# Key norms as two 288-token halves, later store and reload of the solved blocks, and three longer projection stretches in a Hymba/RWKV-7 layer

## The chip, the cores and the metric

The kernel runs on one core of one Trainium2 chip. The metric is device microseconds of one execution. A core has TensorE (PE, the matmuls, with its weight loads shown apart as PEld), VectorE (DVE), ScalarE (ACT), GpSimd (POOL) and SyncE (SP), which in this kernel issues nearly all DMAs. Each of these works through a queue of its own, and engines wait for one another by semaphores. Matmul results go to PSUM, which here is eight banks of 512 float32 per partition.

## The reference, cut to what matters

One layer on 512 tokens plus 16 meta tokens, width 2048:

```python
hn = rmsnorm(h_res, norm_in_g)
P = hn @ w_in                       # 65 column tiles of 128: r k v g (8 each), lora, B C h gc (8 each)
# group A, 16 heads of 64: token shift, decay by a low-rank path, then
kk = (k * k_k) / max(norm(k * k_k over the head), 1e-12)
S_t = S_{t-1} diag(w_t) - (S_{t-1} kk_t)(kk_t * a_t)^T + v_t k_t^T ;  y_t = S_t r_t
y_a = (groupnorm(y) + bonus) * silu(g_r)
# group B: y_b = Bg * causal_conv3(Cg * hc) * silu(g_c)
out = rmsnorm(h_res + concat(y_a, y_b) @ w_out, norm_f_g)[16:]
```

The recurrence over tokens is computed in nine chunks of 64 positions (the 16 meta tokens are padded to a chunk, so a head pair has 576 columns). Within a chunk it needs the inverse of a unit triangular 64x64 matrix for each head and chunk.

## The kernel before, in words

**Projections as filler.** All matmuls that matter in size are float32 products split into high and low parts: three matmuls (high by high, low by high, high by low) for each 128x128 weight tile. `mains` (from L449) is a generator that yields after each projection matmul of the 65 column tiles, in the order of `plan` (L105): lora k0 r0 v0 k1 r1 v1 g0 g1 C0 h0 B0 gc0, then for each later pair of head pairs k r v k r v g g C h B gc, and at the end C h B gc for i = 4 to 7. A column tile uses four quarters of weights (512 columns each); a `wr` load (L134) brings two quarters, ACT casts the high part `wh` (L126), and DVE (even quarters) or POOL (odd quarters) subtracts to get the low part `wl` (L127). Three raw buffers and six buffers each for high and low parts let this run up to six quarters ahead of PE.

**The host clock.** The order of PE's instructions is written out by hand. `fill(ns)` lets the generator run until so many nanoseconds of projection have been emitted, by a price of 0.43 ns a column; the dictionary `FW` holds these stretches. `until(key)` lets it run until a named tile is complete. `later(ns, fn)` emits a DMA when the same clock has advanced by `ns`; it is put behind the latest weight load on SP. The instructions of DVE, ACT, POOL and SP are put in order by the compiler's scheduler, by priority and by its own idea of when operands are there; `ahead()` and the splitting of weights raise the priority.

**One head pair (`prepare`, from L577).** It runs until k of the pair is complete, makes decays (`low_rank`), the operands `ar` and `bk`, and then products of 64 by 128 per head and chunk (`gram`, L631, the Gram blocks), masked on DVE into `gt`. The squares of k (split in `sqh`, `sql`) are summed over each head by a matmul with a two-column 0/1 matrix (L663, L664): these are the key norms `n2`, first 512 columns into a PSUM tile `zn`, then 64 columns into the free end of the ninth Gram block's tile `ze[0]`. Then follows `zb` (L666, L667), a 128-column product for the bonus term. ACT copies the norms to SBUF (L670). They go to DRAM and come back as 72 rows of 16 (`nd`), and the 16x16 diagonal blocks of the triangular matrices come the same way (`d`). DVE inverts all of them in some 40 small steps that end at L739 (`y`). `y` is stored to DRAM (L754) and read back transposed as `xT` and `xo` (L745, L746, both in `load_inverse`). The Gram blocks, keys and values go to `opd` in DRAM meanwhile (`bt`, `vs`, `gt` stashes, L567).

**Two head pairs together (`invert`, from L781).** After a stretch of `FW["solve"]` (`FW["solve_first"]` for the first two head pairs) the 16x16 inverses are combined to 32x32 and to 64x64: a DVE transpose `xn` for each head pair (L794), 64 small matmuls `t` (L801), an ACT copy `ts`, matmuls `z` (L815, L817), DVE copies into `xT` and transposes `xm`, matmuls `t2` (L841), ACT copies `tm`, matmuls `z2` (L856, L860), DVE copies into `xT` (L866), each step followed by a stretch of projection. Then `put_inverse` stores them. After the last two head pairs the stretch is `FW["begin"]`, and the recurrence follows (`recur`, from L888): per chunk `ct` loads (L883), matmuls `rz`, `zs`, `zy`, three stretches of projection, a norm. What is left of the projections runs after it beside the loads of the mixed rows (`split_mix`), and the output projection `o` (L1087) ends the kernel.

**C, h, B, gc** of group B: `u` (POOL, L401) multiplies C by h, ACT takes the first tap of the convolution (`cv`, L403), DVE the other two (L405), POOL multiplies by B (L413), DVE gates (L362, L419).

Of the kernel before, what the change touches and what calls it, by code (L numbers as in the profile page):

```python
# [9 lines left out]
F32 = mybir.dt.float32  # L10
# [8 lines left out]
P = 128  # L19
DM = 2048  # L20
KT = DM // P
SEQ = 512
META = 16
L = SEQ + META
CH = 64
NCH = SEQ // CH + 1
LP = NCH * CH
# [13 lines left out]


FW = dict(
    evac=34, start=1062, lora=2200, gram=8000, gram_b=13500, gram2=5500, misc=2000, v=2000, vt=1000, solve=22500, solve_first=26000,
    tr=3200, lev=3000, cp=4200, out=1500, begin=17000, p=2900, u=2900, s=5200, last=3700, mix=2600,
)


# [28 lines left out]
def hymba_kernel(ctx: ExitStack, tc: tile.TileContext, xt, xtok, w_in, w_out, pv, lup, cst, msk, gf, out):  # L77
    nc = tc.nc
    ctx.enter_context(tc.manual_schedule(engines={mybir.EngineType.PE}))
    cp = ctx.enter_context(tc.tile_pool(name="cp", bufs=1))  # L80
# [16 lines left out]
    def col(off, i=0):  # L97
        return pvt[:, off + i : off + i + 1]
# [56 lines left out]
    pz = ph1.enter_context(tc.tile_pool(name="pz", bufs=2, space=PSUM))  # L155
    pi = ph1.enter_context(tc.tile_pool(name="pi", bufs=1, space=PSUM))
# [5 lines left out]
    def tr(name, dt=F32):  # L162
        return cq.tile([P, LP], dt, tag="tr", name=name, bufs=5)
# [118 lines left out]
    for b in range(2):  # L282
# [5 lines left out]
        out=omm, in0=pvt[:, V_MU : V_MU + 33], scalar1=-1.0, scalar2=1.0, op0=ALU.mult, op1=ALU.add  # L288
    )
    for d, off in (  # L290
# [4 lines left out]
            out=d, in0=pvt[:, off : off + 8], scalar1=0.5, scalar2=None, op0=ALU.mult  # L295
        )
    nc.vector.tensor_scalar(
        out=hv[:, 4], in0=pvt[:, V_KA : V_KA + 8], scalar1=-0.5, scalar2=1.0, op0=ALU.mult, op1=ALU.add
# [183 lines left out]
    def later(ns, fn):  # L482
        pending.append((clock[0] + ns, fn))
        pending.sort(key=lambda e: e[0])
# [30 lines left out]
    def low_rank(i, j, up, w0, name, pad):  # L515
        t = tr(name)
        nc.gpsimd.memset(t[:, META:CH], pad)
        hi, lo = up
        for a, b in ((0, 272), (272, L)):
            z = pz.tile([P, b - a], F32, tag="tz", name=f"{name}_{a}")  # L520
            nc.tensor.matmul(z, hi[:, j], la[:, j, a:b], start=True, stop=False)
            nc.tensor.matmul(z, lo[:, j], la[:, j, a:b], start=False, stop=True)
            with tc.high_priority(offset=AHEAD):
                if a == 0:
                    nc.scalar.activation(t[:, 0:META], z[:, 0:META], AF.Tanh, bias=w0, scale=0.5)
                    nc.scalar.activation(t[:, CH : 5 * CH], z[:, META:272], AF.Tanh, bias=w0, scale=0.5)
                else:
                    nc.scalar.activation(t[:, 5 * CH : LP], z, AF.Tanh, bias=w0, scale=0.5)
            fill(FW["lora"])
        return t  # L530
# [5 lines left out]
    def c3(t):  # L536
        return t.rearrange("p (c s) -> p c s", s=CH)
# [39 lines left out]
    def prepare(i):  # L577
        p = i % 2
# [8 lines left out]
        tz = low_rank(i, 0, up, hv[:, 0, i : i + 1], f"tz{i}", -1.0)  # L587
# [12 lines left out]
            out=bk[:, :, 0], in0=c3(k), scalar=hv[:, 2, i : i + 1], in1=c3(te), op0=ALU.mult, op1=ALU.mult  # L600
# [3 lines left out]
            out=ta, in0=ta, scalar1=hv[:, 3, i : i + 1], scalar2=hv[:, 4, i : i + 1], op0=ALU.mult, op1=ALU.add  # L604
        )
        nc.vector.scalar_tensor_tensor(
            out=ar[:, :, 0], in0=c3(k), scalar=col(V_KK, i), in1=e1[:, :, 0:CH], op0=ALU.mult, op1=ALU.mult
# [8 lines left out]
            out=ar[:, 1:NCH, 1], in0=c3(r), in1=e1[:, 1:NCH, 1 : CH + 1], op=ALU.mult  # L616
        )
        nc.vector.scalar_tensor_tensor(
            out=r, in0=r, scalar=hv[:, 5, i : i + 1], in1=ta[:, CH:LP], op0=ALU.mult, op1=ALU.mult
# [9 lines left out]
        def gram(z, c, c0):  # L629
            for h, hs, ho in heads:  # L630
                nc.tensor.matmul(  # L631
                    z[h][:, c - c0],
                    bk[hs, c, h : h + 2, :].rearrange("p a s -> p (a s)"),
                    ar[hs, c].rearrange("p a s -> p (a s)"),
                    start=True, stop=True,
                )
# [17 lines left out]
        masked(zc, 4, 8)  # L654
        fill(FW["gram2"])

        ze = [pz.tile([P, P + CH], F32, tag="tz", name=f"g{i}_8_{h}") for h in range(2)]
        gram([z[:, 0:P].unsqueeze(1) for z in ze], 8, 8)
        n2 = tr(f"n2{i}")
        zn = pi.tile([2, SEQ], F32, tag="misc", name=f"n2_{i}")  # L660
        zs = ((zn, 0, SEQ), (ze[0][0:2, P : P + CH], SEQ, LP))
        for z, a, b in zs:
            nc.tensor.matmul(z, ones[:, P : P + 2], sqh[:, a:b], start=True, stop=False)  # L663
            nc.tensor.matmul(z, ones[:, P : P + 2], sql[:, a:b], start=False, stop=True)  # L664
# [17 lines left out]
        sx = scr_x[i % 2]  # L682
# [4 lines left out]
        def blocks(t):  # L687
            return bass.AP(tensor=t.tensor, offset=t.offset, ap=[[BLK, 8 * NCH], [CH, 16], [1, 16]])
# [15 lines left out]
        y = cq.tile([NB, 256], F32, tag="y", name=f"y{i}").rearrange("p (s t) -> p s t", t=16)  # L704
# [14 lines left out]
        for m in (2, 4, 8):  # L719
            for b in range(16 // (2 * m)):  # L720
# [4 lines left out]
                    out=pq,  # L725
# [5 lines left out]
                    out=tq.rearrange("p (i j) -> p i j", i=m), in_=pq, op=ALU.add, axis=AX.X  # L731
                )
                nc.vector.tensor_tensor(
                    out=pq,
# [16 lines left out]
                    ),  # L751
                )

        later(20500 if p else 29000, lambda: nc.sync.dma_start(blocks(sx), y))  # L754
        later(22500 if p else 33000, load_inverse)

        for h, hs, ho in heads:
            for b in range(2):
# [6 lines left out]
        v = got["v", i]  # L765
# [244 lines left out]
    for i in range(0, NPAIR, 2):  # L1010
        invert([prepare(i), prepare(i + 1)])
# [56 lines left out]
    last = [[pw.tile([P, 512], F32R, name=f"wlast{a}{j}") for j in range(NL)] for a in range(2)]  # L1068
# [105 lines left out]
    with tc.manual_schedule(engines={mybir.EngineType.DVE, mybir.EngineType.Activation, mybir.EngineType.Pool}):  # L1174
# [9 lines left out]
        for part in range(2):  # L1184
# [3 lines left out]
            if part == 0:  # L1188
                finish(2)
                nc.vector.tensor_tensor(  # L1190
                    out=fv[:, 3, 0:1], in0=fv[:, 3, 0:1], in1=ssq[:, 3, 3:4], op=ALU.add
# [60 lines left out]
```

## Time and profile before

| | |
|---|---|
| median of 3 runs | 1050.98 us (1050.79 to 1051.12) |
| the profiled execution's own time | 1051.02 us |
| its span, first to last instruction | 1049.2 us |
| mean granted TensorE clock | 0.994 |
| projections of `w_in` end, `o` begins | about 861.8 us from the span's start |
| share of 16 DMA engines' time taken by SP's and ACT's queue | 54.6% |

A row of the page's first part gives busy time, share and number of instructions of each engine. A row of the waits gives engine and line, what it waited for, and the total, the number and the longest in us. A row for one tile gives the number of instructions, the least, median and longest duration in ns, and first and last start. A row of the timeline gives start, duration (both us), engine, line, operation, the tiles written and read, and, in brackets, the idle time before it and what ended that. A row of the chain gives start, duration, engine and line. The starts of matmuls are those at which PE took them up; their ends are modelled, so the pace is read from start to start. The SP rows are the issue of a DMA, not its transfer.

### The profile page before, as it was taken

Reading aid. Unit: us, or ns where it says so; the run is one execution under the profiler, and the core shown is the slowest. Engines: PE = TensorE matmul, PEld = TensorE weight load, DVE = VectorE, ACT = ScalarE, POOL = GpSimd, SP = SyncE. Lnnn points to the kernel's source line nnn. Section 1 sums busy time; section 2 is a strip of 40 time slices with the busy share of each in tenths; the row PEclk is TensorE's granted clock in tenths of the full one; section 3 lists DMA queues with packets and bytes.
Section 4 is the critical chain, followed back from the end, with each engine's and each line's share of the span. In section 5 each row is a group of like instructions: output and inputs, shape, how many; then the busy total and the mean of one; then the engine's idle time right before and its main releaser. Section 6 shows DMA issues by size and latency. Waiting matters only on the chain.

```text
span 1049.2 us, 23744 instructions
## 1 busy us (share of the span) xinstructions
PE 1031.6 (98%) x9845; PEld 940.8 (90%) x9845; DVE 580.1 (55%) x1088; ACT 360.0 (34%) x666; POOL 311.1 (30%) x315
## 2 busy tenths in 40 slices
PE   8999998999999999999999999999999999999996
PEld 6999996999998999989999988889898988888885
DVE  6786855569754669753768752444555761212222
ACT  7554313433322434332443232222233342323232
POOL 0132613323222323222323131223233232424132
PEclk8999999999999999999999999999999999999998
DMA  8436565464763273853374748777654958323314
GB/s 292 141 101 166 128 160 145 114 159 103 193 182 114 82 193 84 202 159 114 104 171 103 196 144 291 241 219 221 211 135 150 286 182 296 101 86 95 101 61 161
DMA packets 183404, 167.48 MB, mean 160 GB/s; under 512 B 121472, under 2 KB 143744, under 8 KB 182912
## 3 DMA queue, kind: packets, MB, share of 16 engines
q1 hardware_dynamic: 182720, 164.90, 54.6%
q8 instruction: 77, 1.26, 0.5%
q10 hardware_dynamic: 576, 1.07, 0.3%
q14 instruction: 31, 0.25, 0.1%
HBM read 129.05 MB, written 36.88 MB: 158 GB/s over the span
## 4 chain that ended last, share of the span: by engine, by line
PE 94%; DMA 2%; issue 1%; DVE 1%; POOL 0%; SPq 0%; ACT 0%; DVEq 0%; ACTq 0%; POOLq 0%
PE o L1087 17%; PE ps_v L315 9%; PE ps_g L315 9%; PE ps_k L315 9%; PE ps_gc L315 9%; PE ps_r L315 8%; PE ps_B L315 8%; PE ps_C L315 8%; PE ps_h L315 8%; PE g L631 2%; DMA wq<-in_w_in_dram 1%; PE zs L954 1%; PE zy L958 1%; PE ps_lora L315 1%; PE rz L902 1%
## 5 line engine op out<-in xcount | busy, mean ns | idle before, releaser
L127 POOL TENSOR_TENSOR wl<-wr,wh 128x512 fp32r<-128x512 f32 x150 | 208.8, 1392 | 460.0 <-ACT wh L126 439.6
L126 ACT CAST wh<-wr 128x512 fp32r<-128x512 f32 x312 | 190.0, 618 | 411.7 <-PE o L1087 93.0
L127 DVE TENSOR_TENSOR wl<-wr,wh 128x512 fp32r<-128x512 f32 x162 | 121.7, 756 | 224.4 <-ACT wh L126 223.2
L1087 PE MATMUL o<-wh,m 128*128 128x512 f32 (+1 forms) x484 | 145.2, 384 | 0.0
L1087 PEld LDWEIGHTS o<-wh,m 128*128 128x128 f32 x484 | 89.6, 188 | 21.3
L1087 PE MATMUL o<-wl,m 128*128 128x512 f32 (+1 forms) x242 | 92.6, 389 | 0.0
L315 PE MATMUL ps_h<-xh,wh 128*128 128x258 f32 (+1 forms) x256 | 72.7, 284 | 0.6 <-issue 0.6
L315 PE MATMUL ps_k<-xh,wh 128*128 128x264 f32 x256 | 73.2, 286 | 0.0
L315 PE MATMUL ps_v<-xh,wh 128*128 128x264 f32 x256 | 73.2, 286 | 0.0
L315 PE MATMUL ps_k<-xl,wh 128*128 128x264 f32 x256 | 73.1, 285 | 0.0
L315 PE MATMUL ps_k<-xh,wl 128*128 128x264 f32 x256 | 72.9, 285 | 0.0
L315 PE MATMUL ps_r<-xh,wh 128*128 128x258 f32 (+1 forms) x256 | 72.2, 282 | 0.7 <-ACT wh L225 0.7
L315 PE MATMUL ps_v<-xh,wl 128*128 128x264 f32 x256 | 72.7, 284 | 0.0
L315 PE MATMUL ps_v<-xl,wh 128*128 128x264 f32 x256 | 72.7, 284 | 0.0
L315 PE MATMUL ps_C<-xh,wh 128*128 128x258 f32 (+1 forms) x256 | 72.5, 283 | 0.0
L315 PE MATMUL ps_g<-xl,wh 128*128 128x258 f32 (+1 forms) x256 | 72.4, 283 | 0.0
L315 PE MATMUL ps_h<-xl,wh 128*128 128x258 f32 (+1 forms) x256 | 72.3, 283 | 0.0
L315 PE MATMUL ps_C<-xl,wh 128*128 128x258 f32 (+1 forms) x256 | 72.3, 282 | 0.0
L315 PE MATMUL ps_r<-xh,wl 128*128 128x258 f32 (+1 forms) x256 | 72.1, 282 | 0.0
L315 PE MATMUL ps_r<-xl,wh 128*128 128x258 f32 (+1 forms) x256 | 72.0, 281 | 0.0
L315 PE MATMUL ps_g<-xh,wh 128*128 128x258 f32 (+1 forms) x256 | 71.9, 281 | 0.0
L315 PE MATMUL ps_C<-xh,wl 128*128 128x258 f32 (+1 forms) x256 | 71.9, 281 | 0.0
(274 smaller groups left out, 2715.9 us busy)
## 6 DMA issues: line engine op xcount, KB each, us to landing
wr<-in_w_in_dram SPq DMA_DIRECT2D x127, 512.0 KB
ct<-opd SPq DMA_DIRECT2D x64, 288.0 KB
wr<-in_w_out_dram SPq DMA_DIRECT2D x32, 512.0 KB
opd<-ar SPq DMA_DIRECT2D x8, 576.0 KB
opd<-gt SPq DMA_DIRECT2D x16, 288.0 KB
opd<-bt SPq DMA_DIRECT2D x64, 64.0 KB
xres<-in_xtok_dram SPq DMA_DIRECT2D x4, 768.0 KB
out_dram<-xres SPq DMA_DIRECT2D x6, 512.0 KB
```

The costliest lines, as they stand in the source:

```text
L126: nc.scalar.copy(hi, rq)
L127: eng.tensor_tensor(out=lo, in0=rq, in1=hi.bitcast(F32), op=ALU.subtract)
L315: nc.tensor.matmul(ps[r], ww[:, w], xx[:, kt, a:b], start=(kt == 0 and n == 0), stop=(kt == KT - 1 and n == 2))
L631: nc.tensor.matmul(z[h][:, c - c0], bk[hs, c, h : h + 2, :].rearrange("p a s -> p (a s)"), ar[hs, c].rearrange("p a s -> p (a s)"), start= ...
L902: nc.tensor.matmul(z[e][ho if e else hs, 0, k], t[hs, o : o + CH], t[hs, O_V : O_V + CH] if part else st[hs, 4 * e + k], start=(part == 0 ...
L954: nc.tensor.matmul(d[hs, j], w, x[hs], start=(a == 0), stop=(a == b - 1))
L958: nc.tensor.matmul(d[ho, j], t[hs, o : o + CH], x[hs], start=(a == 0), stop=(a == b - 1))
L1087: nc.tensor.matmul(ps[t + p], mm[:, tk], ww[:, o], start=(jj == 0 and q == 0), stop=(jj == KT - 1 and q == 2))
```

## The change

Three things. The key norms are made in two halves of 288 columns, and the second half goes into the ninth Gram block's tile, which grows from 128+64 to 128+288 columns. The stretches `solve`, `solve_first` and `begin` grow by 2000, 4000 and 2500 ns of the host clock. The store of `y` and the reload of `xT` and `xo` of the odd head pairs are due 2000 ns later, those of head pair 1 by 5000 ns.

```diff
-    evac=34, start=1062, lora=2200, gram=8000, gram_b=13500, gram2=5500, misc=2000, v=2000, vt=1000, solve=22500, solve_first=26000,
-    tr=3200, lev=3000, cp=4200, out=1500, begin=17000, p=2900, u=2900, s=5200, last=3700, mix=2600,
+    evac=34, start=1062, lora=2200, gram=8000, gram_b=13500, gram2=5500, misc=2000, v=2000, vt=1000, solve=24500, solve_first=30000,
+    tr=3200, lev=3000, cp=4200, out=1500, begin=19500, p=2900, u=2900, s=5200, last=3700, mix=2600,
...
-        ze = [pz.tile([P, P + CH], F32, tag="tz", name=f"g{i}_8_{h}") for h in range(2)]
+        ze = [pz.tile([P, P + 288 * (1 - h)], F32, tag="tz", name=f"g{i}_8_{h}") for h in range(2)]
         gram([z[:, 0:P].unsqueeze(1) for z in ze], 8, 8)
         n2 = tr(f"n2{i}")
-        zn = pi.tile([2, SEQ], F32, tag="misc", name=f"n2_{i}")
-        zs = ((zn, 0, SEQ), (ze[0][0:2, P : P + CH], SEQ, LP))
+        zn = pi.tile([2, 288], F32, tag="misc", name=f"n2_{i}")
+        zs = ((zn, 0, 288), (ze[0][0:2, P : P + 288], 288, LP))
         for z, a, b in zs:
             nc.tensor.matmul(z, ones[:, P : P + 2], sqh[:, a:b], start=True, stop=False)
             nc.tensor.matmul(z, ones[:, P : P + 2], sql[:, a:b], start=False, stop=True)
...
-        later(20500 if p else 29000, lambda: nc.sync.dma_start(blocks(sx), y))
-        later(22500 if p else 33000, load_inverse)
+        later((25500 if i == 1 else 22500) if p else 29000, lambda: nc.sync.dma_start(blocks(sx), y))
+        later((27500 if i == 1 else 24500) if p else 33000, load_inverse)
```

## The prediction

> **What bounds the kernel now.** I read the page's busy shares first, then PE's own waits, longest first, then the timelines around the longest of them.
>
> ```profile
> PE 1031.6 (98%) x9845; PEld 940.8 (90%) x9845; DVE 580.1 (55%) x1088; ACT 360.0 (34%) x666; POOL 311.1 (30%) x315
> ```
>
> PE is occupied nearly throughout, so the time is PE's work plus the places where it stands. The change leaves the number of columns that PE multiplies as it is. It can only win what PE loses in standing or in imperfect overlap, and it can lose by making new waits. PE's waits, of which I leave out those of the first 50 us and one of 0.6 us:
>
> ```profile
> PE ps_B L315 <- DVE wl L127: 1.6, 1, 1.6
> ...
> PE ps_gc L315 <- DVE wl L127: 0.9, 1, 0.9
> ...
> PE t L801 <- DVE xn L794: 0.5, 1, 0.5
> PE rz L902 <- DMA ct<-opd: 0.5, 1, 0.5
> ```
>
> Four waits, each once, 3.5 us together. Three of them lie close together in the first inversion; PE's timeline there:
>
> ```profile
> 157.83 0.39 PE L315 MATMUL ps_B<-xl,wh 128*128 128x512 f32 x1
> 159.81 0.50 PE L315 MATMUL ps_B<-xh,wl 128*128 128x512 f32 x1 [1.59 <-DVE wl L127]
> ...
> 165.25 0.39 PE L315 MATMUL ps_gc<-xl,wh 128*128 128x512 f32 x1
> 166.56 0.50 PE L315 MATMUL ps_gc<-xh,wl 128*128 128x512 f32 x1 [0.92 <-DVE wl L127]
> ...
> 168.88 0.69 PE L801 MATMUL t<-xn,gt 64*64 64x64 f32 x32 [0.50 <-DVE xn L794]
> 169.50 0.50 PE L315 MATMUL ps_gc<-xh,wh 128*128 128x512 f32 x1
> 169.84 0.39 PE L315 MATMUL ps_gc<-xl,wh 128*128 128x512 f32 x1
> ```
>
> The reader is to see the restart too: after a wait the next matmul follows 0.34 us later (169.50 to 169.84), where the usual distance for 512 columns is 0.23 us (zb_l below, 85.36 to 85.59). A wait so costs 0.11 us more than its bracket says. Who made PE wait is in the queues of ACT, POOL, DVE and SP at this place:
>
> ```profile
> 155.78 0.72 ACT L403 ACTIVATE cv<-u,pvt 128x512 f32<-128x512 f32 x1 [11.78 <-POOL u L401]
> 156.41 2.17 ACT L126 CAST wh<-wr 128x512 fp32r<-128x512 f32 x4
> ```
> ```profile
> 153.58 2.17 POOL L401 TENSOR_TENSOR u<-u,hh 128x514 f32<-128x514 f32 x1 [10.80 <-DVE hh L334]
> ```
> ```profile
> 150.82 0.43 DVE L334 TENSOR_TENSOR hh<-ps_h,rs 128x258 f32<-128x258 f32 x1 [3.09 <-PE ps_h L315]
> ...
> 153.09 0.41 DVE L334 TENSOR_TENSOR hh<-ps_h,rs 128x256 f32<-128x256 f32 x1
> ...
> 158.00 1.76 DVE L127 TENSOR_TENSOR wl<-wr,wh 128x512 fp32r<-128x512 f32 x1
> 165.21 0.69 DVE L334 TENSOR_TENSOR b<-ps_B,rs 128x512 f32<-128x512 f32 x1 [5.46 <-PE ps_B L315]
> 165.82 2.38 DVE L127 TENSOR_TENSOR wl<-wr,wh 128x512 fp32r<-128x512 f32 x2
> 168.12 0.70 DVE L794 STREAM_TRANSPOSE xn<-xT 128x512 f32<-128x512 f32 x1
> ```
> ```profile
> 155.32 0.30 SPq L754 DMA_DIRECT2D sx<-y  x1
> 155.72 0.51 SPq L134 DMA_DIRECT2D wr<-in_w_in_dram  x1
> ```
>
> **First wait (1.59).** Four casts stand on ACT behind the convolution's first tap `cv`, which stands 11.78 us for POOL's `u`, which waits for the second half of `hh`; that half came 2.3 us after the first because steps of the `y` chain stood between them on DVE. **Second (0.92).** The next `wl` stands on DVE behind `b`, which cannot start before PE is through with B. **Third (0.50).** The transposition of the second head pair stands behind those two `wl`.
>
> The queue that the change touches is SP's. It stood for `y` before the store:
>
> ```profile
> SPq L754 <- DVE y L739: 14.3, 4, 7.4
> ```
>
> Here the longest case, 7.4 us, ended with the store at 155.32, and the weight load behind it went out at 155.72. But the weights of the first two waits had been loaded before (the casts at 156.41 waited for ACT's own queue, not for a DMA). So the visible block on SP is not what PE waited for in the first two waits. I hold this against the easy reading of the profile.
>
> **The norms.** Columns: 2x512 and 2x64 before, 4x288 after, 1152 both times. PE around the first of eight:
>
> ```profile
> 84.75 0.39 PE L664 MATMUL n<-sq_l,ones 128*2 128x512 f32 x1
> 84.98 0.19 PE L663 MATMUL g<-sq_h,ones 128*2 128x64 f32 x1
> ...
> 85.04 0.48 PE L666 MATMUL zb<-rk_h,ones 128*128 128x512 f32 x1
> 85.36 0.40 PE L667 MATMUL zb<-rk_l,ones 128*128 128x512 f32 x1
> 85.59 0.28 PE L315 MATMUL ps_r<-xl,wh 128*128 128x258 f32 x1
> ```
>
> The two 64-column matmuls take 0.06 us together (84.98 to 85.04), in proportion to the 0.23 us of 512 columns. But `zb` with the high part takes 0.32 us to the next start, 0.09 more than its twin: 0.06 us of matmul is not long enough to hide the load of its 128 weight columns. A 288-column matmul lasts 0.23 x 288/512 = 0.13 us, so after the change the load is hidden as it is behind every 258-column projection. Win: about 0.08 us x 8 = **0.6 us**, bounds 0 and 0.7.
>
> A rule speaks against this term. The Trainium skill, "TensorE: Matmul & The Clock Gate", section "Back-to-back issue gap", gives for a single warm matmul a gap of N/2.4 + 2.5 ns. By it the four cost 2x215.8 + 2x29.2 = 490 ns before and 4x122.5 = 490 ns after: nothing won, and the sum below would come to 1049.8. It does not describe this trace, whose step from zb to zb is 320 and not 216 ns.
>
> ACT copies the norms:
>
> ```profile
> L670 ACT COPY n<-n x8: 575/576/576, 85.2 to 572.1; 2x512 f32<-2x512 f32 x8
> L670 ACT COPY n<-g x8: 197/197/197, 85.7 to 572.5; 2x64 f32<-2x64 f32 x8
> ```
>
> The three figures are the least, the median and the longest in ns. (576-197)/448 is 0.85 ns a column, so 387 ns for 288: 774 against 773 ns. The first can start 0.2 us earlier, the masking of the shared bank ends about where it did. Nothing on PE: 0.
>
> **The longer stretches.** They move projections from behind a point to ahead of it. Until where? The next `prepare` begins with `until` k. Rows of the chain:
>
> ```profile
> 182.40 0.68 PE t L841 x50
> ...
> 194.28 1.31 PE ps_r L315 x11
> ...
> 318.00 0.68 PE t L841 x50
> ...
> 345.38 1.31 PE ps_r L315 x11
> ...
> 791.91 2.55 PE ps_h L315 x20
> ...
> 861.77 177.06 PE o L1087 x798
> ```
>
> After `t2` at 182.40 the first inversion has `lev` 3000 and `out` 1500 of the host clock left; 10.57 us of that clock (48x512x0.43) are about 48 x 0.23 = 11.1 us of PE, a factor of 1.05. That and 1.6 us of small products end near 189. k2 is complete at 194.28, so `until` already supplies some 5 us; the added 4000 (4.2 us) only shorten that. In the next inversion 345.38 - 318.00 leaves some 20 us for an added 2.1; the third is alike. So the first three additions are swallowed and prepare(2), (4) and (6) stay where they are. Only the last, 2000 + 2500, moves the recurrence, by 4.7 us of projection. The tail has room: the recurrence ends near 791.9 (the last two rows) and `o` starts at 861.8, of which `last` and `mix` need 4x3.7+8x2.6 = 35.6, so some 30 us stay. Cost 0.
>
> What comes closer together: `z2` of the first inversion to the first low-rank product, by 4 us to some 5. That product needs a PSUM bank which eight DVE copies must have read:
>
> ```profile
> 322.87 2.40 DVE L866 COPY xT<-z 32x128 f32<-32x128 f32 x8 [0.48 <-PE z L860]
> ```
>
> 2.4 + 1 us of matmuls and waiting fit in; if two `wl` come between (2.38 above), PE stands up to 1 us. I take 0.
>
> **Store and reload.** For head pair 1 the store moves on SP from ahead of the load of the next weights to behind that and the one after; SP no longer stands for `y`, and the weight load of 155.72 can go out near 148. The second load waits for a raw buffer that is split at 159.8, so the store goes at about 160, the reload at 162 to 165, landing near 167. The `t` stage moves by 4.2 us to about 172. So `xn` is no longer last: the third wait, 0.50 + 0.11 = **0.6 us**, goes. In the other pairs store, reload and use move together.
>
> The **first two waits** (1.59 + 0.92 + 2x0.11 = 2.7 us) hang on the order in which the scheduler put `cv`, `b` and the splits; what comes before the store in program order is unchanged by the edit, so I take that they stay: 0, the other bound -2.7.
>
> **The start of the recurrence.**
>
> ```profile
> 644.78 0.33 PE L902 MATMUL rz<-ct 64*64 64x64 f32 x4 [0.48 <-DMA ct<-opd]
> ```
>
> 4.7 us more projection ahead of `rz` cover this wait: 0.48 + 0.11 = **0.6 us**.
>
> **Sum.** -0.6 - 0.6 - 0.6 = -1.8 us on the profiled execution's 1051.0 (span 1049.2 and 1.8 around it), which is within 0.1 of the median of 1050.98: **1049.2 us**. A measurement of this kernel tells about 0.2%, 2.1 us, from no change, so this forecast lies just inside "same".
>
> **Rivals.**
> A: the new order on SP also changes the scheduler's order on ACT and DVE, and the first two waits go as well. For it: `wl` at 165.82 waited for nothing but its place. Against: the queue ahead of the store is the same. 1049.2 - 2.7 = **1046.5**.
> B: the edit doesn't do what it says: the waits around the first inversion only change places, `xn` or a split late by as much, and just the norms and the recurrence's start are won, or the norms alone: 1049.8 to **1050.4**.
> C, slower: in the three later inversions, which have no PE wait now, the `t` stage stands 2 us later beside h and B. If the copies and transposes of the inversion come ahead of `hh` there, the splits fall behind `cv` on ACT as in the first one. Price: the first wait, 1.7 us, in each of three: 1049.2 + 5.1 = **1054.3**. It decides as soon as `cv` stands so long that ACT's six quarters of lead (16.6 us of PE) are used up; all three must do so, or two of them with the second wait as well (5.4), for a slower verdict.
>
> **How the numbers follow.** Forecast 0.42 (own range 1048.3 to 1050.0, of which 0.13 falls below 1048.9), A 0.30, B 0.08, C 0.20. Faster by over 0.2%: 0.13 + 0.30 = 0.43. Within: 0.29 + 0.08 = 0.37. Slower: 0.20. The range takes in A with 0.5 of margin and half of C: 1046.0 to 1053.5.
>
> **What would show it.** `zb` of high parts followed after 0.23 us by its twin, eight times. No bracket at `rz` of chunk 0 and none at `t`. L754 gone from SP's long waits, the weight load behind it near 148. If ps_B and ps_gc still wait for `wl`, the forecast holds; if not, A. New waits of ps_C, ps_h, ps_B or ps_gc after 290 us mean C. Wrong would be the whole if the recurrence moved by some 13 us instead of 4.7, or if PE's steps of the projections changed.

## The result and the profile after

The changed kernel takes 1062.9 us (median of 4 runs, 1062.2 to 1064.44) against 1050.88 us for the one before. The ratio is 1.0117, with a 95% interval of 1.0099 to 1.0134: slower by 1.2%. The profiled execution's span is 1061.5 us, 12.3 more than before.

PE's waits in the changed kernel; the rows left out belong to the first 50 us, the last gives the start of the recurrence:

```profile
PE t L801 <- DVE xn L794: 11.8, 4, 7.7
...
PE ps_gc L315 <- DVE wl L127: 0.9, 1, 0.9
PE ps_B L315 <- DVE wl L127: 0.6, 1, 0.6
PE rz L902 <- DMA ct<-opd: 0.4, 1, 0.4
```

The wait for `xn` was there once with 0.5 us. It is there four times now, once in each inversion, with 11.8 us, and the longest is 7.7. So the place of the loss is the first small matmuls of the inversions. To see how much each costs, the chain of the two kernels is compared at the same instructions. Two rows of the kernel before that the prediction does not show, each the start of a head pair's Gram blocks:

```profile
118.02 1.99 PE g L631 x32
...
260.81 1.20 PE g L631 x17
```

and the rows of the changed kernel:

```profile
118.74 1.99 PE g L631 x32
...
203.00 1.31 PE ps_r L315 x11
...
269.39 1.99 PE g L631 x32
...
355.45 1.31 PE ps_r L315 x11
...
874.06 177.06 PE o L1087 x798
```

From the Gram blocks at 118 to the end of k2 (the start of that `ps_r`) it was 194.28 - 118.02 = 76.3 us and is 84.3: +8.0, in the first inversion. From 260.81 to 345.38 it was 84.6 and is 86.1: +1.5, in the second; the third has the same distance, and the fourth the same wait. The span had lost 0.7 before 118 us, in the loads at the start, which the change does not touch (PE's first projections start at 21.92, 21.09 before). After `o` begins nothing differs.

**The first inversion.** SP's queue in the changed kernel. In the text I count the weight loads from 0, two for each column tile; the load at 159.48 is w26.

```profile
159.48 0.35 SPq L134 DMA_DIRECT2D wr<-in_w_in_dram  x1
159.88 0.40 SPq L754 DMA_DIRECT2D sx<-y  x1
169.03 2.05 SPq L134 DMA_DIRECT2D wr<-in_w_in_dram  x2
171.13 0.60 SPq L745 DMA_DIRECT2D xT<-sx  x1
...
173.12 0.64 SPq L746 DMA_DIRECT2D xo<-sx  x1
173.86 1.73 SPq L134 DMA_DIRECT2D wr<-in_w_in_dram  x2
```

The store goes at 159.88, and the reload could follow some 2.6 us later, as it did in the kernel before, whose store went at 155.32:

```profile
157.90 0.60 SPq L745 DMA_DIRECT2D xT<-sx  x1
```

But in the changed kernel w27 and w28 stand ahead of it, and w27 has to wait for a raw buffer: SP stands from 160.3 to 169.0 with the reload behind it. The reload is issued from 171.13 to 173.76, and then shares the DMA engines with four weight loads. DVE and PE:

```profile
179.24 0.71 DVE L794 STREAM_TRANSPOSE xn<-xT 128x512 f32<-128x512 f32 x1 [5.14 <-DMA xT<-sx]
```
```profile
180.01 1.13 PE L801 MATMUL t<-xn,gt 64*64 64x64 f32 x32 [7.73 <-DVE xn L794]
...
182.09 0.63 PE L315 MATMUL ps_gc<-xh,wl 128*128 128x512 f32 x1
182.51 0.63 PE L315 MATMUL ps_gc<-xh,wh 128*128 128x512 f32 x1
```

After the wait the matmuls are 0.42 us apart (182.09 to 182.51), not 0.23. The windows of the same stretch show why; the columns are us, busy time of PE, PEld, DVE, ACT and POOL, granted clock, DMA share, GB/s:

```profile
171.60:180.00 8.40, 0.68 (x33) 0.54 (x32) 1.40 (x2) 1.14 (x2) 1.84 (x2) 0.84 1.00 243
180.00:184.20 4.20, 4.19 (x40) 3.45 (x41) 0.00 (x0) 1.08 (x2) 0.00 (x0) 0.51 0.14 54
184.20:190.00 5.80, 5.80 (x88) 4.71 (x87) 3.56 (x8) 1.20 (x2) 0.00 (x0) 1.00 0.02 4
```

During the wait the DMA engines are full (1.00), and after it the granted clock is 0.51 for 4.2 us. Seven matmuls then cost 0.2 us more each and the 32 of `t` 0.4 more, some 1.8 us on top of the 7.7. Less the 1.6 us by which the old waits shrank (`ps_B` from 1.59 to 0.60, `t` without its 0.50 and the restart behind it) that is 7.9 of the 8.0.

The Trainium skill, "TensorE: Matmul & The Clock Gate", section "What's actually happening", says that the array falls to half its clock after an idle window of about 3.4 us and returns after a busy one. The trace agrees: 0.51 behind 8.4 us of near idleness, and no such slow rows behind the waits of 0.6 to 1.4 us (the granted clock is 1.00 from 160 to 166 us and from 317 to 320).

**The later inversions.** DVE in the second one before the change and after it:

```profile
302.84 0.70 DVE L794 STREAM_TRANSPOSE xn<-xT 128x512 f32<-128x512 f32 x1
306.62 0.69 DVE L127 TENSOR_TENSOR wl<-wr,wh 128x512 fp32r<-128x512 f32 x1 [3.08 <-ACT wh L126]
307.23 0.42 DVE L334 TENSOR_TENSOR hh<-ps_h,rs 128x258 f32<-128x258 f32 x1
```
```profile
314.21 0.43 DVE L334 TENSOR_TENSOR hh<-ps_h,rs 128x258 f32<-128x258 f32 x1 [7.49 <-PE ps_h L315]
314.55 1.28 DVE L127 TENSOR_TENSOR wl<-wr,wh 128x512 fp32r<-128x512 f32 x2
315.75 0.70 DVE L794 STREAM_TRANSPOSE xn<-xT 128x512 f32<-128x512 f32 x1
```
```profile
316.51 0.69 PE L801 MATMUL t<-xn,gt 64*64 64x64 f32 x32 [1.36 <-DVE xn L794]
```

Before, the transposition stood ahead of `hh`. Now it stands behind the first half of `hh`, for which DVE waits 7.49 us until PE is through with that half of h, and behind two splits. The reload had landed: its last part is issued by 307.9, and from 314 to 316 the DMA engines have nothing to move (share 0.00). PE stands 1.36 us in each of three inversions.

### The profile page after: what moved, and what is told of

The parts are those of the page before. It is cut to its first block, busy times and chain, and to the rows that moved or that the text cites. A ratio compares the mean times of both kernels' runs of the same rounds, so it can differ in the third digit from the quotient of the medians.

```text
span 1061.5 us, 23736 instructions
## 1 busy us (share of the span) xinstructions
PE 1034.3 (97%) x9845; PEld 943.7 (89%) x9845; DVE 575.5 (54%) x1088; ACT 360.2 (34%) x666; POOL 302.3 (28%) x315
## 3 DMA queue, kind: packets, MB, share of 16 engines
q10 hardware_dynamic: 576, 1.07, 0.3%
## 4 chain that ended last, share of the span: by engine, by line
PE 90%; DMA 3%; issue 2%; DVE 1%; SPq 1%; POOL 1%; ACT 0%; DVEq 0%; POOLq 0%; ACTq 0%
PE o L1087 17%; PE ps_v L315 9%; PE ps_k L315 9%; PE ps_g L315 8%; PE ps_r L315 8%; PE ps_gc L315 8%; PE ps_h L315 8%; PE ps_B L315 8%; PE ps_C L315 7%; PE g L631 2%; DMA wq<-in_w_in_dram 1%; PE zs L954 1%; PE zy L958 1%; PE ps_lora L315 1%; PE rz L902 1%
## 5 line engine op out<-in xcount | busy, mean ns | idle before, releaser
L127 POOL TENSOR_TENSOR wl<-wr,wh 128x512 fp32r<-128x512 f32 x150 | 201.0, 1340 | 459.7 <-ACT wh L126 441.4
L315 PE MATMUL ps_h<-xh,wl 128*128 128x258 f32 (+1 forms) x256 | 72.2, 282 | 0.0
```

The lines of the kernel that those rows point to most:

```text
L127: eng.tensor_tensor(out=lo, in0=rq, in1=hi.bitcast(F32), op=ALU.subtract)
L315: nc.tensor.matmul(ps[r], ww[:, w], xx[:, kt, a:b], start=(kt == 0 and n == 0), stop=(kt == KT - 1 and n == 2))
```

## The experiments

My theory after the traces: two places in queues make the loss, the reload's on SP (first inversion) and the transposition's on DVE (the others), and the norms are a small win. Rivals: (1) the norms' longer hold of the Gram block's bank upsets the solve; (2) the longer stretch costs by itself; (3) the cost grows in proportion to the delay. Ratios are to the kernel before on the same chip, where its median was 1051.39 us (e1 to e4), 1051.88 (e5 to e8) or 1052.0 (e9 to e11).

**e1, norms alone.** The three lines of the norms from the diff above, constants as before.

> The kernel before with nothing but the norms in two halves. Theory (the loss comes from where the reloads and transpositions stand in the queues of SP and DVE): the norms win 0.12 to 0.14 us on TensorE in each of eight pairs, 1.0 us together, so 1049.8 against 1050.9. Rival 1 (the longer hold of the Gram block's bank upsets the solve): 1055 or more, with a wait at t.

Measured 1049.84 us, ratio 0.9988 (0.9978 to 0.9998). Rival 1 falls. The wait that was PE's longest at the first inversion, 1.6 us at `ps_B`, is shorter too:

```profile
PE ps_B L315 <- DVE wl L127: 0.6, 1, 0.6
```

**e2, constants alone.** The opposite half of the diff.

> All stretches and due times of the change, the norms as before. Theory: the change's loss in full plus the norms' win that is missing, 1062.9 + 1.0 = 1063.9, t waiting for xn 7 to 8 us once and 1.4 us three times. Rival 1: near 1051.

Measured 1064.07 us, ratio 1.0123 (1.0108 to 1.0139), `t` waiting 11.5 us in four places, the longest 7.4. The whole loss is in the constants. This run also has the old norms with a store that no longer holds up SP: the weight load that went out behind the store at 155.72 goes out at 148.22, and `ps_B` still waits as long as before (and `ps_gc` 0.9):

```profile
148.22 0.35 SPq L134 DMA_DIRECT2D wr<-in_w_in_dram  x1
```
```profile
PE ps_B L315 <- DVE wl L127: 1.6, 1, 1.6
```

**e3, head pair 1 early.**

```diff
-        later((25500 if i == 1 else 22500) if p else 29000, lambda: nc.sync.dma_start(blocks(sx), y))
-        later((27500 if i == 1 else 24500) if p else 33000, load_inverse)
+        later((20500 if i == 1 else 22500) if p else 29000, lambda: nc.sync.dma_start(blocks(sx), y))
+        later((22500 if i == 1 else 24500) if p else 33000, load_inverse)
```

> The change with store and reload of head pair 1 due as before (20500 and 22500), all else changed. Theory: the reload stands ahead of the two weight loads that it stood behind, the 7.7 us at the first inversion and the slower clock after it go, and the three waits of 1.4 us stay: 1050.9 - 1.0 (norms) + 4.5 (three waits) - 1.5 (shorter waits at the first inversion) = about 1053. Rival 2 (the longer stretch solve_first itself costs it): about 1062.

Measured 1052.55 us, ratio 1.0010 (1.0001 to 1.0019). The 7.7 us are gone; three waits of up to 1.4 us at `t` stay (4.1 together). With solve_first still at 30000, rival 2 falls for the first inversion.

**e4, solve short.** `solve=22500`, and pairs 3, 5 and 7 due at 20500 and 22500 as before, all else as changed.

> The change with the stretch solve and the due times of head pairs 3, 5 and 7 as before, all else changed. Theory: the three waits of 1.4 us go, the one of 7.7 us stays: 1062.9 - 4.5 = 1058.4. Rival 2: the three follow from the first, so 1062 to 1063 as long as that stays.

Measured 1058.4 us, ratio 1.0066 (1.0050 to 1.0081); one wait of 8.0 us at `t`, no others. The two losses are separate and add, within the intervals.

**e5 and e6, the place or the delay.** The change with head pair 1 due half a microsecond of the host clock apart; the diff is e5's, e6 has 23500 and 25500:

```diff
-        later((25500 if i == 1 else 22500) if p else 29000, lambda: nc.sync.dma_start(blocks(sx), y))
-        later((27500 if i == 1 else 24500) if p else 33000, load_inverse)
+        later((23000 if i == 1 else 22500) if p else 29000, lambda: nc.sync.dma_start(blocks(sx), y))
+        later((25000 if i == 1 else 24500) if p else 33000, load_inverse)
```

> The change, with store and reload of head pair 1 due at 23000 and 25000 in place of 25500 and 27500: the store then comes just ahead of the weight load w26 on SP, the reload ahead of w27. Theory (the place in SP's queue decides, not the delay): no wait of 7.7 us, time as in e3, about 1052.5. Rival 3 (every later due time costs in proportion: half of the 5000 moved, so half of the 10.3 us between e3 and the change): 1057.7.

> The same with 23500 and 25500, half a microsecond of the host clock later: the store falls behind w26, the reload behind w27 and w28. Theory: the wait of 7 to 8 us is back in full, 1062 to 1063. Rival 3: 1058.7.

Measured: e5 1052.65 us, ratio 1.0005 (0.9996 to 1.0015), with the three waits of up to 1.4 us alone at `t`; e6 1062.91 us, ratio 1.0103 (1.0087 to 1.0119), with a longest wait of 8.2 us there. SP in e5, then in e6:

```profile
158.49 0.35 SPq L134 DMA_DIRECT2D wr<-in_w_in_dram  x1
158.94 0.60 SPq L745 DMA_DIRECT2D xT<-sx  x1
...
168.04 3.51 SPq L134 DMA_DIRECT2D wr<-in_w_in_dram  x3
```
```profile
158.26 0.35 SPq L134 DMA_DIRECT2D wr<-in_w_in_dram  x1
158.66 0.40 SPq L754 DMA_DIRECT2D sx<-y  x1
167.83 2.05 SPq L134 DMA_DIRECT2D wr<-in_w_in_dram  x2
169.93 0.60 SPq L745 DMA_DIRECT2D xT<-sx  x1
```

In both, SP stands for w27, which goes out at about the same time (168.04 and 167.83). In e5 the reload is ahead of it, in e6 behind. 500 ns of due time cost 10 us; nothing is in proportion, so rival 3 falls. Why the compiler's scheduler lets w27 and w28 pass the reload once the store stands behind w26 cannot be read from a trace, and stays open.

**e7, solve at 24000.** The change with head pair 1 early, `solve=24000`, and pairs 3, 5 and 7 due at 22000 and 24000.

> The change with head pair 1 due as before and solve at 24000, 500 less than the change, with store and reload of pairs 3, 5 and 7 at 22000 and 24000. The transposition then stands ahead of both halves of hh on DVE. Theory: the three waits of 1.4 us vanish, 1052.6 - 4.5 = 1048.1. Rival 3 (cost in proportion to the stretch, three quarters of it left): 1051.4.

Measured 1047.64 us, ratio 0.9956 (0.9943 to 0.9970), no wait at `t` at all. Again an edge: with 500 ns less, in the stretch and in the due times, the transposition stands ahead of `hh`.

**e8, what is left without the losses.** The norms in halves, `solve_first=30000`, `begin=19500`; `solve` and all due times as before.

> The norms in halves, solve_first 30000 and begin 19500; solve and all due times as before. Theory: the wait of 0.5 us at t (first inversion) and those of 0.5 to 0.9 us at rz go, no new ones: 1049.8 - 0.6 - 0.7 = 1048.5, under both kernels. Rival 2 (the stretch solve_first costs by itself): above 1051.

Measured 1047.35 us, ratio 0.9953 (0.9940 to 0.9965): faster than both kernels. The waits at `t` and at `rz` are gone.

**e9, solve long, due times old.** e8 with `solve=24500`.

> The kernel of e8 with solve at 24500, all due times of store and reload as before. Theory (the stretch puts the transposition behind the first half of hh on DVE): that order is there, with one split between instead of two, so three waits of about 0.7 us at t: 1047.4 + 2.5 = 1049.9. Rival 4 (the later reload makes the three waits): none, 1047.4.

Measured 1050.79 us, ratio 0.9986 (0.9977 to 0.9995), three waits at `t` of 2.3 us together and one at `rz` of 0.4. DVE in the second inversion:

```profile
303.39 0.43 DVE L334 TENSOR_TENSOR hh<-ps_h,rs 128x258 f32<-128x258 f32 x1 [7.49 <-PE ps_h L315]
303.73 0.68 DVE L127 TENSOR_TENSOR wl<-wr,wh 128x512 fp32r<-128x512 f32 x1
304.33 0.70 DVE L794 STREAM_TRANSPOSE xn<-xT 128x512 f32<-128x512 f32 x1
```

One split instead of two, and half the wait. So the stretch alone puts the transposition behind `hh`: rival 4 falls, and for these three inversions rival 2 holds, by way of DVE's queue. The second split comes between only where the due times are later too, as in e3; that other half of the wait is not the stretch's alone.

**e10, due times late, solve old.** e8 with pairs 3, 5 and 7 due at 22500 and 24500.

> The kernel of e8 with store and reload of head pairs 3, 5 and 7 due 2000 later and the stretch solve as before. Theory: the order on DVE stays as before (transposition ahead of hh), but the reload lands up to 2 us later where t had 0.3 us to spare: three waits of 1 to 2 us for a DMA, 1051 to 1054. Rival 5 (the reload's due time costs nothing, since in the kernel before the store waited 2 us for y anyway): 1047.4.

Measured 1046.84 us, ratio 0.9947 (0.9932 to 0.9962). My theory missed here: no wait at `t`. DVE does wait for the reload now, but early enough:

```profile
300.39 0.71 DVE L794 STREAM_TRANSPOSE xn<-xT 128x512 f32<-128x512 f32 x1 [2.43 <-DMA xT<-sx]
...
305.33 0.42 DVE L334 TENSOR_TENSOR hh<-ps_h,rs 128x258 f32<-128x258 f32 x1
```

It ends at 301.1, and `t` starts at 301.9 without a bracket. At the old stretch the later due times of these three pairs are free; at the longer one, e9 against e3, they go with a wait of 1.36 us in place of 0.76.

**e11, head pair 1 at 22000 and 24000.** e8 with these due times, so that SP issues w25, the load behind the store, ahead of it.

> The kernel of e8 with head pair 1's store and reload due at 22000 and 24000, so that SP issues w25 before it comes to the store and the reload still goes ahead of w27. Theory: SP's wait for y is worth nothing to TensorE, 1047.4 within 0.5. Rival 6 (the weight load w25 behind the store is what makes ps_gc wait for its split): the 0.9 us at ps_gc go, 1046.4.

Measured 1047.07 us, ratio 0.9952 (0.9940 to 0.9965), and `ps_gc` still waits 0.9 us, `ps_B` 0.6. In e8 SP stood only 1.4 us before this store, and e11 sends w25 out 1.2 us earlier (152.98 after 154.19), so this is a small test. The large one is e2, where that load was 7.5 us earlier than in the kernel before and neither wait changed: SP's stand of 7.4 us for `y` was worth nothing to PE.

## Why the prediction was wrong

**Store and reload, the step that failed.** The prediction put the store at about 160 (159.88 in the trace), "the reload at 162 to 165, landing near 167", and took 0.6 us as won. The `t` stage came when forecast (171.58, for about 172), but the reload went at 171.1 to 173.8 and the second head pair's `xn` could start only at 179.24. I had seen that w26 waits for a raw buffer, and did not ask the same of the two loads behind it, which on SP came ahead of the reload. So the wait of 0.5 us became one of 7.7 with a slow clock behind it. e3 and e5 take it away by the place of store and reload alone; of the two the reload counts, since in e6 its store is out 11 us before it (158.66 and 169.93).

**The longer stretches, costed at 0.** That `until` swallows them holds for PE's order: the two kernels differ in length between Gram blocks and k only by the waits and the slow clock behind the longest. But the cover named for them was projection on PE. The transposition needs DVE, and a `t` stage 2 us later falls behind `hh` in DVE's queue, 1.36 us three times (e4, e7, e9). Rival C had named the place (h, in the three later inversions) and the price (1.7 each), with another mechanism: splits late behind `cv`. Those splits were not late for PE.

**"In the other pairs store, reload and use move together"**: the reload did keep ahead of its use there, and e10 shows that at the old stretch even its move alone was free.

**The first two waits**, taken as staying: `ps_gc` stayed at 0.92; `ps_B` fell from 1.59 to 0.60. e1 and e2 show that the norms made this, not the store. POOL's `u` in the changed kernel:

```profile
154.08 1.30 POOL L401 TENSOR_TENSOR u<-u,hh 128x514 f32<-128x514 f32 x1 [10.39 <-DVE hh L334]
```

It took 2.17 us before, and 2.17 in e2, 1.30 in e1. With the norms in halves the `y` chain is further on, and its last long product stands ahead of the second half of `hh` on DVE, not beside `u`; that POOL is slow because of that product fits these four runs but was not tested by itself. The reading that SP's stand for `y` was not what PE waited for is confirmed by e2. The weight load behind the store went out at 154.08, not near 148 as forecast, without a longer wait on PE.

**The norms**, 0.08 us each. PE around the first in the changed kernel:

```profile
85.75 0.30 PE L664 MATMUL g<-sq_l,ones 128*2 128x288 f32 x1
85.88 0.39 PE L666 MATMUL zb<-rk_h,ones 128*128 128x512 f32 x1
86.11 0.40 PE L667 MATMUL zb<-rk_l,ones 128*128 128x512 f32 x1
86.35 0.28 PE L315 MATMUL ps_r<-xl,wh 128*128 128x258 f32 x1
```

`zb` is followed by its twin after 0.23 us, as forecast, and the win there is 0.32 - 0.23 = 0.09. From the first norm matmul to the next projection it is 0.99 us, 1.07 before (0.08). The term was right in mechanism and size; the shorter wait at `ps_B` came on top, and e1's 1.2 per mille fits the sum of 0.7 and 1.0 us (1.6 per mille) within its interval.

**The start of the recurrence**, 0.6 us won: the recurrence moved by 4.9 us, 4.7 forecast (its first `rz` starts at 660.89, 643.26 before, and 12.7 of these 17.6 us had been lost ahead of it), but in the changed kernel 0.4 us of the wait stays. SP before:

```profile
632.55 2.92 SPq L883 DMA_DIRECT2D ct<-opd  x6
...
639.08 0.32 SPq L420 DMA_DIRECT2D mixd<-cv  x1
```

and in the changed kernel:

```profile
645.32 0.41 SPq L883 DMA_DIRECT2D ct<-opd  x1
650.48 0.33 SPq L134 DMA_DIRECT2D wr<-in_w_in_dram  x1
651.83 0.33 SPq L420 DMA_DIRECT2D mixd<-cv  x1
652.26 10.27 SPq L883 DMA_DIRECT2D ct<-opd  x15
```

Before, six `ct` loads went ahead of the store of `mixd`, which waits for DVE; now one does. The longer stretch was given, and the loads moved behind the wait. With `solve` at its old length (e8, e10) six go ahead again and the wait is gone. The order explains only part: with one load ahead the wait is 0.4 us in e5 and e9, 0.2 in e6, and e3 has none that is listed.

Without the two queue places the win is more than the 1.8 us forecast: e8 wins 4.9 us (3.7 to 6.3) by its ratio, and its profiled span is 3.6 us shorter than that of the kernel before. The three wins as forecast and the 1.0 us at `ps_B` are 2.8 of that; where the rest comes from was not settled.

## What to carry to other kernels

In this kernel a due time on SP's queue bought or lost places, not nanoseconds: before moving a DMA, list what it will then stand behind, and for each of those ask what it waits for itself. The same holds for a stage that is moved by giving PE more filler: its first DVE or ACT step can land behind other instructions on that engine, which wait for PE. A long wait on TensorE can cost more than its length: behind the 7.7 us the granted clock was 0.51 and 1.8 us more went, while behind the waits of up to 1.4 us it was 1.00.

## What the runs showed that I had not expected

Half a microsecond of host clock (e5 to e6) is worth 10.3 us, and as little (e7 at 24000, the change at 24500) decides over three waits. The granted clock of 0.51 lasted 4.2 us behind the wait of 7.7 us and cost 1.8 us. And cutting the norms' matmuls in other pieces, with the same columns in total, shortened a wait some 30 us later (`ps_B`, 1.59 to 0.60).
